# Ten of 32 destination blocks summed from gathered rows, 64-slot halves in pass 2, and one 384-wide product per source block

## The chip, the cores and the metric

The kernel runs on one core of a Trainium2 chip. The metric is device time in microseconds (us), smaller is better. Each kernel was timed in several rounds beside the kernel before on the same chip. A profiled execution has a span of its own, which is within about 1% of the median of the timed runs.

Names used below: PE multiplies matrices (PEld is its weight load), DVE does vector arithmetic, ACT does copies and activations, POOL issues the indirect DMAs, SP issues the other DMAs. PSUM is the memory into which PE writes its sums.

## The reference

```python
def reference(node_features, edge_index_src, edge_index_dst):     # 4096 nodes x 128, 65536 edges
    output = np.zeros((num_nodes, dim), dtype=np.float32)
    for i in range(len(edge_index_src)):
        output[edge_index_dst[i]] += node_features[edge_index_src[i]]
    return output
```

## The kernel before

The 4096 nodes are 32 blocks of 128. Two sorting passes, built from one-hot products, bring the edges into an order in which each pair of a destination block and a source block has its own columns. Then every destination block is *dense*: for each of 32 source blocks, PE makes the 128 x 128 count matrix of edges from two one-hots (`blocks`), and multiplies it with the features of the source block (`product`). Features are held as three bf16 parts whose sum is the float32 value, hence three products.

```python
    def blocks(k, oh, a):                       # PE -> psa, ACT copies it to a
        psa = ps.tile([P, 1024], F32, name="psa", tag="psA")
        for i in range(8):
            s = k * 8 + i
            PE.matmul(out=psa[:, i * P:(i + 1) * P], lhsT=oh[0][:, s, :], rhs=oh[1][:, s, :],
                      start=True, stop=True)
        S.copy(out=a[:, k * 8:k * 8 + 8, :], in_=psa[:].rearrange("p (s m) -> p s m", s=8))

    def product(k, a, pso):
        for s in range(k * 8, k * 8 + 8):
            for v in range(3):
                PE.matmul(out=pso[:, :P], lhsT=a[:, s, :], rhs=x3[:, s, v, :],
                          start=s == 0 and v == 0, stop=s == NB - 1 and v == 2)

    def finish(d, pso):
        res = sb2.tile([P, P], F32, name="res")
        S.copy(out=res[:], in_=pso[:, :P])      # ACT
        nc.sync.dma_start(out=out[d * P:(d + 1) * P, :], in_=res[:])
    # ... (cut) pass2(g), a generator, prepares the keys of the next 8 destination blocks
    for d in range(NB):
        # ... (cut) a new generator gen every 8 blocks
        oh = onehots(d)                         # two DVE instructions, 128 x 4096
        if gen is not None:
            next(gen, None)                     # one step of pass 2 for the next group
        a = sb2.tile([P, NB, P], BF16, name="a", tag="t1")
        pso = ps.tile([P, 512], F32, name="pso", tag="pso")
        for k in range(4):
            blocks(k, oh, a)
            if prev is not None:
                product(k, prev[1], prev[2])    # of the block before
        if prev is not None:
            finish(prev[0], prev[2])
        prev = (d, a, pso)
```

The instructions of each engine are issued in the order of this program. So what stands first on DVE is done first, even if a later instruction could already run.

## Time and profile before

| | before |
|---|---|
| median of timed runs | 508.5 us |
| span of the profile, mean granted PE clock | 507.9 us, 0.818 |
| first count-matrix product of the dense stage | at 180.4 us |
| from there to the end | 327.5 us |
| period of a settled dense block | 7.15 us |

From the page of the kernel before: the chain that ended last by engine, and its costliest groups. The columns of a group are line, engine, operation, output and inputs, shapes and count; then busy us and mean ns of one; then the idle us of the engine just before the group, and what ended most of it.

```profile
PE 59%; DVE 31%; issue 5%; ACT 3%; DMA 1%; DVEq 0%; ACTq 0%
...
L293 PE MATMUL pso<-x,a 128*128 128x128 bf16 x3072 | 200.2, 224 | 0.0
...
L176 DVE TENSOR_TENSOR p<-iota,rank 128x3072 bf16<-128x3072 uint16 (+1 forms) x38 | 90.8, 2426 | 24.3 <-PE ps L251 24.3
L276 DVE TENSOR_TENSOR oh<-iotas,slo 128x4096 bf16<-128x4096 uint16 x32 | 73.2, 2289 | 45.1 <-PE psa L286 45.1
L286 PE MATMUL psa<-oh 128*128 128x128 bf16 x1024 | 81.8, 226 | 1.3 <-ACT a L288 1.3
...
L232 PE MATMUL psr<-cum,identb 128*128 128x192 bf16 x128 | 20.2, 354 | 32.8 <-DVE cum L229 32.8
```

PE has 59% of the chain. Before the dense one-hots `oh`, DVE sits idle for 45.1 us in all *waiting for PE*, and PE hardly waits for anything before `psa` (1.3 us): DVE is ahead, PE sets the pace.

A settled block in the timeline of the kernel before (start us, length us, engine, line and operation; in brackets the idle time before it and its releaser):

```profile
461.68 2.29 DVE L276 TENSOR_TENSOR oh<-iotas,slo 128x4096 bf16<-128x4096 uint16 x1 [2.65 <-PE psa L286]
...
463.06 0.27 ACT L298 COPY res<-pso 128x128 f32<-128x128 f32 x1 [0.37 <-PE pso L293]
...
463.27 1.50 PE L293 MATMUL pso<-x,a 128*128 128x128 bf16 x24
...
463.89 2.28 DVE L276 TENSOR_TENSOR oh<-iota,dlo 128x4096 bf16<-128x4096 uint16 x1
...
464.61 0.61 PE L286 MATMUL psa<-oh 128*128 128x128 bf16 x8
...
470.21 0.27 ACT L298 COPY res<-pso 128x128 f32<-128x128 f32 x1 [0.37 <-PE pso L293]
```

The two results `res` leave 7.15 us apart. In between PE never stops, and the one-hots of the next block (461.68 to 466.17) are made while PE works on this one. The result is taken out of PSUM by ACT, so DVE does not wait for it.

### The profile page before, as it was taken

The numbers are of one execution on the slowest core, as the hardware profiler recorded it, in microseconds if no ns is written. First come the engines' busy times: TensorE is split into PE (matmuls) and PEld (weight loads), VectorE is DVE, ScalarE is ACT, GpSimd is POOL, SyncE is SP. The second block draws the span as 40 slices with busy tenths as digits, with TensorE's granted clock in tenths as the row PEclk, the third lists the DMA queues.
The fourth block names the chain that finished last, engine by engine and source line by source line (L and its number), as shares of the span: only waits on it lengthen the run. The fifth ranks groups of instructions, "written<-read, shape, count | busy, mean of one in ns | idle before, by whom it ended". The sixth has DMA issues, their size and how long they took to land.

```text
span 507.9 us, 12335 instructions
## 1 busy us (share of the span) xinstructions
PE 375.5 (74%) x5709; PEld 358.5 (71%) x5709; DVE 366.0 (72%) x429; ACT 163.1 (32%) x213; POOL 1.5 (0%) x10
## 2 busy tenths in 40 slices
PE   0607574610339283999999499999949999999997
PEld 0305574610238283999999499999949999999996
DVE  5697999735859899566789956678995666655630
ACT  1001000045000050332656133265613326665652
POOL 1000000000000000000000000000000000000000
PEclk9957766665665596987999798799979879999999
DMA  5000000011000000000000000000000000000000
GB/s 165 1 0 1 1 1 0 1 43 41 0 0 1 2 1 5 8 6 3 12 14 8 5 8 6 3 12 13 8 5 8 7 2 13 13 9 12 12 13 14
DMA packets 9109, 6.05 MB, mean 12 GB/s; under 512 B 608, under 2 KB 8800, under 8 KB 9056
## 3 DMA queue, kind: packets, MB, share of 16 engines
q1 hardware_dynamic: 8912, 4.72, 3.3%
q8 instruction: 45, 0.74, 0.6%
q10 hardware_dynamic: 144, 0.52, 0.3%
q14 instruction: 8, 0.07, 0.0%
HBM read 3.15 MB, written 2.10 MB: 10 GB/s over the span
## 4 chain that ended last, share of the span: by engine, by line
PE 59%; DVE 31%; issue 5%; ACT 3%; DMA 1%; DVEq 0%; ACTq 0%
PE pso L293 32%; PE psa L286 11%; DVE p L176 9%; DVE cum L228 5%; PE ps L251 5%; PE psr L232 4%; DVE oh L276 4%; PE psb L219 3%; DVE cum L229 3%; DVE v L141 2%; DVE cum L152 2%; ACT x L202 2%; DVE xf L204 2%; PE psr L160 2%; PE psb L131 2%
## 5 line engine op out<-in xcount | busy, mean ns | idle before, releaser
L293 PE MATMUL pso<-x,a 128*128 128x128 bf16 x3072 | 200.2, 224 | 0.0
L293 PEld LDWEIGHTS <-a 128*128 128x128 bf16 x3072 | 185.3, 100 | 0.0
L288 ACT CAST a<-psa 128x1024 bf16<-128x1024 f32 x128 | 129.2, 1013 | 87.3 <-PE psa L286 87.0
L176 DVE TENSOR_TENSOR p<-iota,rank 128x3072 bf16<-128x3072 uint16 (+1 forms) x38 | 90.8, 2426 | 24.3 <-PE ps L251 24.3
L276 DVE TENSOR_TENSOR oh<-iotas,slo 128x4096 bf16<-128x4096 uint16 x32 | 73.2, 2289 | 45.1 <-PE psa L286 45.1
L286 PE MATMUL psa<-oh 128*128 128x128 bf16 x1024 | 81.8, 226 | 1.3 <-ACT a L288 1.3
L276 DVE TENSOR_TENSOR oh<-iota,dlo 128x4096 bf16<-128x4096 uint16 x32 | 73.1, 2284 | 0.0
L286 PEld LDWEIGHTS <-oh 128*128 128x128 bf16 x1024 | 65.9, 101 | 1.7 <-issue 1.6
L251 PE MATMUL ps<-ov,p 128*128 128x32 bf16 x768 | 50.2, 238 | 6.7 <-DVE p L176 6.0
L251 PEld LDWEIGHTS <-p 128*128 128x128 bf16 x768 | 46.1, 120 | 10.2 <-DVE p L176 10.2
L190 PE MATMUL psm<-v,p 128*128 128x64 bf16 x512 | 31.7, 239 | 23.6 <-DVE p L176 23.1
L190 PEld LDWEIGHTS <-p 128*128 128x128 bf16 x512 | 30.6, 123 | 24.7 <-DVE p L176 24.7
L232 PE MATMUL psr<-cum,identb 128*128 128x192 bf16 x128 | 20.2, 354 | 32.8 <-DVE cum L229 32.8
L232 PEld LDWEIGHTS <-identb 128*128 128x128 bf16 x128 | 18.3, 144 | 34.7 <-issue 21.8
L219 PE MATMUL psb<-ov,before 128*128 128x256 bf16 x96 | 14.5, 322 | 35.2 <-DVE ov L215 35.2
L219 PEld LDWEIGHTS <-before 128*128 128x128 bf16 x96 | 10.9, 115 | 38.2 <-issue 26.0
L228 DVE TENSOR_TENSOR cum<-cum,ov 128x256 bf16<-128x256 bf16 x92 | 26.8, 291 | 4.4 <-ACT cum L222 1.4
L160 PE MATMUL psr<-cum,identb 128*128 128x264 bf16 x64 | 9.7, 323 | 17.5 <-DVE cum L157 17.5
L204 DVE TENSOR_TENSOR xf<-xf,x 128x1024 f32<-128x1024 f32 x8 | 9.8, 1226 | 17.3 <-ACT x L202 17.3
L160 PEld LDWEIGHTS <-identb 128*128 128x128 bf16 x64 | 7.1, 112 | 20.2 <-DVE cum L157 17.9
L254 ACT CAST pa<-ps 128x128 bf16<-128x128 f32 x8 | 2.1, 266 | 53.2 <-PE ps L251 53.2
L236 ACT CAST rank<-psr 128x192 bf16<-128x192 f32 x8 | 2.5, 377 | 51.7 <-PE psr L232 51.7
(47 smaller groups left out, 146.7 us busy)
## 6 DMA issues: line engine op xcount, KB each, us to landing
xf<-in_node_features_dram SPq DMA_DIRECT2D x4, 512.0 KB, 5.1
out_dram<-res SPq DMA_DIRECT2D x32, 64.0 KB, 1.5
raw<-in_edge_index_src_dram ACTq DMA_DIRECT2D x1, 512.0 KB, 5.1
raw<-in_edge_index_dst_dram SPq DMA_DIRECT2D x1, 512.0 KB, 4.9
```

The source lines that it names most:

```text
L160: PE.matmul(out=psr[:, :HJ * NCH], lhsT=identb[:], rhs=cum1[:, js, :, b, :].rearrange("p j q l -> p (j q) l"), start=b == 0, stop=b == NB - 1)
L176: V.tensor_tensor(out=dst.rearrange("p i (m k) -> p i m k", k=2), in0=iota[:, None, :].to_broadcast([P, n, P]).rearrange("p i (m k) -> p i ...
L190: PE.matmul(out=psm[:, l * 64:(l + 1) * 64], lhsT=p1[:, j * 4 + l, :], rhs=v1[q][:, j, :, :, l].rearrange("p k b -> p (k b)"), start=j == ...
L204: V.tensor_tensor(out=xf[:], in0=xf[:], in1=x3[:, i:i + 8, v, :], op=OP.subtract)
L219: PE.matmul(out=psb2[:, :NB * GD], lhsT=before[:], rhs=oh2[:, c], start=c == 0, stop=c == NCH - 1)
L228: V.tensor_tensor(out=cum2[:, c], in0=cum2[:, c - 1], in1=oh2[:, c - 1], op=OP.add)
L232: PE.matmul(out=psr[:, :NCH * GD], lhsT=identb[:], rhs=cum2[:, :, s, :], start=s == 0, stop=s == NB - 1)
L251: PE.matmul(out=ps2[:, (d % 4) * NB:(d % 4 + 1) * NB], lhsT=p2[:, c, :], rhs=v2[:, c, :, d], start=c == 0, stop=c == NCH - 1)
L276: V.tensor_tensor(out=dst.rearrange("p i (m k) -> p i m k", k=2), in0=io[:, None, :].to_broadcast([P, NB, P]).rearrange("p i (m k) -> p i ...
L286: PE.matmul(out=psa[:, i * P:(i + 1) * P], lhsT=oh[0][:, s, :], rhs=oh[1][:, s, :], start=True, stop=True)
L288: S.copy(out=a[:, k * 8:k * 8 + 8, :], in_=psa[:].rearrange("p (s m) -> p s m", s=8))
L293: PE.matmul(out=pso[:, :P], lhsT=a[:, s, :], rhs=x3[:, s, v, :], start=s == 0 and v == 0, stop=s == NB - 1 and v == 2)
```

## The change

Intent: fewer dense blocks. The source rows of ten destination blocks are fetched from memory by indirect DMA and added up with small one-hot products, on a queue and an engine (POOL) that did next to nothing before (1.5 us). The other 22 stay dense, with one product of 384 columns in place of three of 128. Pass 2 works with two halves of 64 slots, with half the cumulative adds and narrower one-hots, in eight smaller steps; the counts of pass 1 move from DVE to PE. The core of the diff (most of pass 1 is cut):

```diff
+    def gather(d, q):                                   # 60 tiles, 240 indirect DMAs
+        t = xg.tile([P, 4, 3 * P], BF16, name="rows", tag="xg")
+        for l in range(4):
+            G.indirect_dma_start(
+                out=t[:, l, :], out_offset=None, in_=x3d[:, :],
+                in_offset=bass.IndirectOffsetOnAxis(ap=gidx[:, place(q).start + l, d:d + 1], axis=0))
+        rows[d, q] = t
+    def gather_sum(d, q):
+        oh = sb2.tile([P, 4, P], BF16, name="ohg", bufs=6)
+        onehot(oh[:], gkey[:, place(q), d, :], 4)
         ...
+        for l in range(4):
+            PE.matmul(out=psg[d][:, :3 * P], lhsT=oh[:, l, :], rhs=t[:, l, :],
+                      start=q == 0 and l == 0, stop=q == NQ - 1 and l == 3)
+        if q == NQ - 1:
+            finish(d, psg.pop(d))
     def finish(d, pso):
-        S.copy(out=res[:], in_=pso[:, :P])
+        V.tensor_reduce(out=res[:], in_=pso[:, :3 * P].rearrange("p (v f) -> p f v", v=3),
+                        op=OP.add, axis=AX.X)
     ... pass 2, per destination block d of the group:
-                p2 = sb2.tile([P, NCH, P], BF16, name="p2")
-                onehot(p2[:], rank2[:, d], NCH)
+            p2 = p2b[d % 2]
+            for h in range(2):
+                cs = slice(h * NH, (h + 1) * NH)
+                onehot(p2[:, cs, h * 64:h * 64 + 64], rank2[:, d, cs], NH, 64)
     ... product:
-            for v in range(3):
-                PE.matmul(out=pso[:, :P], lhsT=a[:, s, :], rhs=x3[:, s, v, :], ...)
+            PE.matmul(out=pso[:, :3 * P], lhsT=a[:, s, :],
+                      rhs=x3[:, s, :, :].rearrange("p v f -> p (v f)"), ...)
     ... the dense loop:
+            oh = onehots(g, i)
+            while done < -(-STEPS * (i + 1) // gd):
+                next(gen, None)
+                done += 1
             for k in range(4):
                 blocks(k, oh, a)
                 if prev is not None:
                     product(k, prev[1], prev[2])
+                if prev is not None and k == 3:
+                    finish(prev[0], prev[2])
+            add_up(n0 + (len(order) - n0) * slot // slots)      # gather() and gather_sum()
```

`finish` is now a DVE instruction. In DVE's order it stands ahead of the one-hots of the next block.

## The prediction

> **What bounds the kernel now.** Span 507.9 us. By the chain of waits in time order and the timeline: 0-104 us first pass, DVE-bound (one-hot p 6.0 us plus two spreads of 1.62 us per quad, 9.0 us a quad); to 125 us the x split, ACT and DVE in turn; to 167 us the first second-pass group, exposed; then 340 us for 32 dense blocks, PE-bound. A settled dense block costs PE 7.15 us: four times eight block products (0.45 us) and 24 x 128-wide products (1.34 us, 55.8 ns each). Three groups also carry a second pass and take 89 us instead of 57. DVE makes the two one-hots (oh, 4.49 us) ahead and waits for PE (45.1 us).
>
> **What the change moves.**
> - Dense blocks: 32 to 22. Products 96 x 128 wide become 32 x 384 wide: the 128x384 matmuls here run at 160 ns warm, so PE per block is still about 7.0 us. It saves almost nothing by itself.
> - The result is now summed by a DVE reduce (0.55 us for 384 columns, as fmax) instead of an ACT copy. In DVE's order it stands BEFORE the next block's one-hots, and waits for the last product. DVE then does reduce 0.55, two gather one-hots (estimate 0.42 each from the 3072 and 4096 sizes), oh 4.49; PE can't start the next block until that ends. So PE and DVE alternate: 7.0 + 6.0 = 13.0 us a block, against 7.15.
> - The Trainium skill, "TensorE: Matmul & The Clock Gate", Part 1, says an idle window of about 3.4 us halves the PE clock. This trace agrees: after a gap of 6.86 us, 32 matmuls of 192 columns took 5.07 us, 158 ns each, then full speed. The new gap (6 us, 1.3 us of gather products inside) will cost an estimated 0.5 to 2 us per block.
> - Pass 2 halves: p2 3072 elements (1.72 us) to twice 768 (estimate 1.15 us); cum adds 23 to 11. But p2 and its products stand between oh and the block products: estimate 15 us exposed per later group.
> - Pass 1: cumulative counts go to PE (172 matmuls) and ACT copies. Each odd step waits for the previous step's copy, so a pair costs about 1.9 us warm: two halves of 21-30 us, the second ahead of the first move products. I estimate pass 1 ends at 148 us (before: 125 including the split), dense work starts near 178 (before 167).
> - 240 indirect DMAs on POOL. No trace here times one; "DMA: Bandwidth & Descriptors", latency table, gives about 1 us to first byte. From about 84 us they fit unless one costs over 1.8 us.
>
> **Sum.** 178 + 22 x 13.0-15 + 31 (p2) + 10 (eight gather reduces) + 13 (first and last) = 518-562. Since such a change was presumably tuned, I shade down: 527 us, 8 in 10 within 470-580. Faster 0.27, same 0.17, slower 0.56.
>
> **What would show it.** Per dense block a period of 13-15 us, PE idle some 5-6 us, released by DVE oh; DVE idle before the reduce res<-pso, released by PE; granted clock below the 0.9-1.0 of the old dense stage; PE busy down by about 80 us without span; count stage over 45 us.
>
> **What would make it wrong.** An indirect DMA above 1.8 us (POOL busy throughout, PE waiting for rows: slower still), or stalls of POOL under DVE; a shorter gap than computed, or pass 1 well under 140 us (faster); the clock staying full (518 or less).

## The result and the profile after

| | before | after |
|---|---|---|
| median of timed runs | 508.5 us | 608.0 us |
| span, mean granted PE clock | 507.9 us, 0.818 | 604.1 us, 0.793 |
| first count-matrix product | 180.4 us | 228.4 us |
| from there to the end | 327.5 us | 375.7 us |
| period of a late dense block | 7.15 us | 15.4 us |
| POOL busy | 1.5 us | 344.4 us |

The ratio is 1.196 (95% interval 1.189 to 1.202). A ratio here is the mean time of one kernel's fast runs over that of the other's fast runs of the same rounds, so it is not quite the ratio of the medians quoted. The prediction, 527 us within 470 to 580, was wrong in size: the loss was foreseen as the likelier side, but 608 us lies outside the range. So 100 us are to be explained, 81 more than predicted.

From the page of the kernel after, the chain by engine and the groups that answer to those above (line numbers are those of the new file; 239 is the line of a helper that makes all one-hots):

```profile
PE 43%; DVE 25%; another core or an unknown queue 13%; issue 9%; ACT 5%; POOL 2%; DMA 1%; DVEq 0%; ACTq 0%
...
L286 POOL DMA_INDIRECT rows<-x3d,gidx x240 | 310.9, 1295 | 212.8 <-PE psg L300 99.0
L434 PE MATMUL pso<-x,a 128*128 128x384 bf16 x704 | 152.1, 368 | 0.0
...
L307 DVE TENSOR_REDUCE res<-pso 128x128 f32<-128x384 f32 x22 | 12.3, 557 | 191.0 <-PE pso L434 173.7
L428 PE MATMUL psa<-oh 128*128 128x128 bf16 x704 | 64.8, 244 | 50.9 <-DVE oh L239 45.3
...
L239 DVE TENSOR_TENSOR oh<-iotas,slo 128x4096 bf16<-128x4096 uint16 x22 | 50.2, 2283 | 0.0
```

The direction of the waiting has turned. DVE sits idle for 191.0 us before its reduces, nearly all until PE ends a product, and PE waits 45.3 us for DVE's one-hots. Each waits for the other in turn. PE's products fell from 200.2 us for 32 blocks to 152.1 us for 22, but nothing of that shows in the span.

One late block in the timeline of the kernel after:

```profile
494.25 0.56 DVE L307 TENSOR_REDUCE res<-pso 128x128 f32<-128x384 f32 x1 [9.76 <-PE pso L434]
494.72 0.75 DVE L239 TENSOR_TENSOR ohg<-iota,gkey 128x512 bf16<-128x512 uint16 x2
...
495.19 1.47 PE L300 MATMUL psg<-rows,ohg 128*128 128x384 bf16 x8 [2.03 <-DVE ohg L239]
495.39 2.28 DVE L239 TENSOR_TENSOR oh<-iotas,slo 128x4096 bf16<-128x4096 uint16 x1
...
497.59 2.28 DVE L239 TENSOR_TENSOR oh<-iota,dlo 128x4096 bf16<-128x4096 uint16 x1
...
499.93 0.62 PE L428 MATMUL psa<-oh 128*128 128x128 bf16 x8 [3.27 <-DVE oh L239]
...
500.39 1.95 PE L434 MATMUL pso<-x,a 128*128 128x384 bf16 x8
...
507.30 1.46 PE L434 MATMUL pso<-x,a 128*128 128x384 bf16 x8
...
509.68 0.56 DVE L307 TENSOR_REDUCE res<-pso 128x128 f32<-128x384 f32 x1 [9.81 <-PE pso L434]
```

The reduce at 494.25 had waited 9.76 us for PE. Only then come the gather one-hots and the one-hots of the next block, and PE's next `psa` starts at 499.93, after 3.27 us idle. PE is done at 508.8 us by its record, yet the reduce that waits for it starts at 509.68. From reduce to reduce it is 15.4 us (14.5 to 16.9 in the last full blocks). This is the alternation the prediction describes.

There is a second thing that it does not describe. Here is PE before the dense stage, with POOL beside it, in the timeline of the kernel after:

```profile
192.12 0.95 POOL L286 DMA_INDIRECT rows<-x3d,gidx  x1 [0.30 <-issue]
193.00 0.30 PE L397 MATMUL ps<-v,p2b 128*128 128x32 bf16 x3 [1.08 <-issue]
...
193.37 0.95 POOL L286 DMA_INDIRECT rows<-x3d,gidx  x1 [0.30 <-issue]
193.75 0.20 PE L397 MATMUL ps<-v,p2b 128*128 128x32 bf16 x1 [0.46 <-issue]
...
194.47 0.29 PE L397 MATMUL ps<-v,p2b 128*128 128x32 bf16 x3 [0.51 <-issue]
194.62 0.94 POOL L286 DMA_INDIRECT rows<-x3d,gidx  x1 [0.30 <-issue]
195.18 0.20 PE L397 MATMUL ps<-v,p2b 128*128 128x32 bf16 x1 [0.42 <-issue]
195.87 0.95 POOL L286 DMA_INDIRECT rows<-x3d,gidx  x1 [0.30 <-issue]
...
196.59 0.30 PE L397 MATMUL ps<-v,p2b 128*128 128x32 bf16 x3 [1.20 <-issue]
```

PE issues matmuls by ones to threes (the count at the end of the line) with gaps of 0.4 to 1.2 us. The releaser is "issue": the profile shows no semaphore that PE waits for, and its operands are ready. Meanwhile POOL issues one indirect DMA every 1.25 us. In all, PE idles 22.0 us in this way in the kernel after, and never in the kernel before.

The trace has another sign of it. Of the PE instructions of the kernel after that signal another engine, 63 of 425 have their next signal on record over 0.3 us later than the end that the trace models for them; in the kernel before 0 of 207 do. I call these *late completions*. Overlapping ones merged, they last 89.8 us in all in this trace. (An end is modelled and the time includes stalls off the critical path, so this is a detector and not a cost. It also counts too much: where there are many indirect DMAs, some signals have no record. The trace of the kernel after holds 405, that of x6, with the same 425 instructions, 428. A missing one is read as late until the next.) A check that needs no such record is the ACT copy of `psa`: in 17 of 88 cases in the kernel after it starts over 0.5 us later than both PE's modelled end and ACT's own last work, 34.5 us in all, and in none of 128 in the kernel before.

### The profile page after: what moved, and what is told of

It reads as the page before. It is cut to its first block, busy times and chain, and to the rows that moved or that the text cites. A ratio compares the mean times of both kernels' runs of the same rounds, so it can differ in the third digit from the quotient of the medians.

```text
span 604.1 us, 7564 instructions
## 1 busy us (share of the span) xinstructions
PE 379.6 (63%) x3151; PEld 251.2 (42%) x3151; DVE 294.9 (49%) x491; ACT 131.2 (22%) x182; POOL 344.4 (57%) x263
## 3 DMA queue, kind: packets, MB, share of 16 engines
q0 software_dynamic: 11520, 23.61, 15.5%
## 4 chain that ended last, share of the span: by engine, by line
PE 43%; DVE 25%; another core or an unknown queue 13%; issue 9%; ACT 5%; POOL 2%; DMA 1%; DVEq 0%; ACTq 0%
PE pso L434 21%; DVE oh L239 13%; PE psa L428 8%; PE psc L191 4%; PE ps L397 3%; PE psg L300 2%; DVE ohg L239 2%; ACT cum L192 2%; PE psm L252 2%; POOL rows L286 2%; PE psr L384 2%; DVE oh L143 1%; DVE cum L377 1%; ACT x L163 1%
## 5 line engine op out<-in xcount | busy, mean ns | idle before, releaser
L286 POOL DMA_INDIRECT rows<-x3d,gidx x240 | 310.9, 1295 | 212.8 <-PE psg L300 99.0
L434 PE MATMUL pso<-x,a 128*128 128x384 bf16 x704 | 152.1, 368 | 0.0
L430 ACT CAST a<-psa 128x1024 bf16<-128x1024 f32 x88 | 88.3, 1015 | 249.9 <-PE psa L428 193.8
L300 PE MATMUL psg<-rows,ohg 128*128 128x384 bf16 x240 | 60.8, 394 | 86.9 <-DVE ohg L239 59.8
L307 DVE TENSOR_REDUCE res<-pso 128x128 f32<-128x384 f32 x22 | 12.3, 557 | 191.0 <-PE pso L434 173.7
L428 PE MATMUL psa<-oh 128*128 128x128 bf16 x704 | 64.8, 244 | 50.9 <-DVE oh L239 45.3
L434 PEld LDWEIGHTS <-a 128*128 128x128 bf16 x704 | 73.7, 110 | 47.3 <-issue 20.1
L397 PE MATMUL ps<-v,p2b 128*128 128x32 bf16 x528 | 34.2, 233 | 26.9 <-DVE p2b L239 14.3
L239 DVE TENSOR_TENSOR oh<-iotas,slo 128x4096 bf16<-128x4096 uint16 x22 | 50.2, 2283 | 0.0
L239 DVE TENSOR_TENSOR oh<-iota,dlo 128x4096 bf16<-128x4096 uint16 x22 | 50.2, 2283 | 0.0
L397 PEld LDWEIGHTS <-p2b 128*128 128x128 bf16 x528 | 30.4, 122 | 32.0 <-DVE p2b L239 16.1
L239 DVE TENSOR_TENSOR p<-iota,rank 128x2816 bf16<-128x2816 uint16 x24 | 37.4, 1618 | 5.7 <-issue 3.0
L252 PEld LDWEIGHTS <-p 128*128 128x128 bf16 x512 | 31.1, 121 | 10.1 <-DVE p L239 7.5
L165 POOL TENSOR_TENSOR xf<-xf,x 128x1024 f32<-128x1024 f32 x8 | 29.0, 3646 | 8.4 <-ACT x L163 8.4
```

What stands on the lines that cost most here:

```text
L165: G.tensor_tensor(out=xf[i][:], in0=xf[i][:], in1=x3[:, i * BX:(i + 1) * BX, v, :], op=OP.subtract)
L239: V.tensor_tensor(out=dst.rearrange("p i (m k) -> p i m k", k=2), in0=io.rearrange("p i (m k) -> p i m k", k=2), in1=keys2[:, :, None, :]. ...
L252: PE.matmul(out=psm[:, l * 64:(l + 1) * 64], lhsT=p1[:, l % 2, j, :], rhs=v1[q][:, j, :, :, l].rearrange("p k b -> p (k b)"), start=j == j ...
L286: G.indirect_dma_start(out=t[:, l, :], out_offset=None, in_=x3d[:, :], in_offset=bass.IndirectOffsetOnAxis(ap=gidx[:, place(q).start + l, ...
L300: PE.matmul(out=psg[d][:, :3 * P], lhsT=oh[:, l, :], rhs=t[:, l, :], start=q == 0 and l == 0, stop=q == NQ - 1 and l == 3)
L307: V.tensor_reduce(out=res[:], in_=pso[:, :3 * P].rearrange("p (v f) -> p f v", v=3), op=OP.add, axis=AX.X)
```

## The experiments

Two theories were open from the start. *Order*: the reduce on DVE stands ahead of the next one-hots and makes PE and DVE alternate. *Gathers*: the indirect DMAs hold up PE, POOL or the rows. Seventeen kernels were run. Kernels marked "wrong" give a wrong result but do the same kinds of work. The kernel before took 508.7 to 509.6 us beside them. The table gives medians; "late" is the merged time of late completions in the profiled run, too large where records are missing, and "issue" is the time that PE idles there with no releaser known.

| run | base | edit | us | ratio | late, us | issue, us |
|---|---|---|---|---|---|---|
| x1_reduce_later | after | reduce behind next one-hots | 577.7 | 1.127 | 115.1 | 51.0 |
| x2_no_gather | after | 24 of 240 gathers | 555.8 | 1.089 | 6.1 | 0 |
| x3_before_wide | before | 384-wide, DVE reduce first | 723.5 | 1.419 | 0 | 0 |
| x4_before_wide_late | before | 384-wide, reduce later | 543.4 | 1.066 | 0 | 0 |
| x5_both | after | x1 and x2 | 478.5 | 0.939 | 4.8 | 0 |
| x6_sp_rows | after | plain DMAs, SP queue | 548.9 | 1.078 | 0 | 0 |
| x7_pool_rows | after | plain DMAs, POOL queue | 551.4 | 1.081 | 0 | 0 |
| x8_rows256 | after | a third of the bytes | 611.7 | 1.199 | 88.5 | 23.2 |
| x9_consecutive | after | consecutive rows | 605.7 | 1.190 | 73.3 | 26.2 |
| x10_wide_after_gen | before | x4, reduce later still | 514.1 | 1.007 | 0 | 0 |
| x11_halves_wide | before | x10 and halves | 6625 | 13.0 | | |
| x12_half | x1 | 132 gathers | 499.4 | 0.977 | 29.3 | 10.6 |
| x13_halves_mended | before | x11 mended | 469.3 | 0.921 | 0 | 0 |
| x14_halves_alone | before | halves only | 469.6 | 0.926 | 0 | 0 |
| x15_one_in_four | x1 | 60 indirect, 180 plain | 478.4 | 0.939 | 0 | 0 |
| x16_memset_between | x1 | memset between gathers | 575.3 | 1.131 | 102.4 | 45.0 |
| x17_plain_between | x12 | plain DMA between gathers | 494.9 | 0.971 | 36.2 | 0 |

### Order and gathers, one at a time and both

x1 undoes only the order: `finish` of a dense block is emitted after the next block's one-hots. Correct.

```diff
+    pend = []
+    def flush():
+        for p in pend:
+            finish(*p)
+        pend.clear()
 ...
             oh = onehots(g, i)
+            flush()
 ...
-                    finish(prev[0], prev[2])
+                    pend.append((prev[0], prev[2]))
```

> The kernel after, with only the order changed on DVE: the reduce of a dense block (and of a gathered block where it can wait) is given to DVE after the next block's one-hots instead of before them. Theory A (PE and DVE alternate because of that order): the settled dense slot falls from 15.4 us to 9 to 11 us, PE no longer waits for oh, the time falls by 70 to 110 us to 500-540 us. Rival B (the excess is stalls that come with the gathers, whatever the order): under 25 us gained, 580 us or more.

Measured 577.7 us: 30 us better, short of what order alone foretold. Late completions grew to 115.1 us, and the late copies of `psa` from 34.5 to 70.2 us. With the alternation gone, the fastest blocks take 8.3 to 9.6 us. Six take 24 to 43 us; the same six take 14 to 23 us in x5 below, so not all of that is the gathers. The timeline of x1 shows one such stall:

```profile
442.97 0.61 PE L428 MATMUL psa<-oh 128*128 128x128 bf16 x8 [1.27 <-ACT a L430]
...
445.89 0.95 POOL L286 DMA_INDIRECT rows<-x3d,gidx  x1 [0.30 <-issue]
...
446.81 0.48 PE L434 MATMUL pso<-x,a 128*128 128x384 bf16 x1 [0.82 <-issue]
447.14 0.94 POOL L286 DMA_INDIRECT rows<-x3d,gidx  x1 [0.30 <-issue]
...
447.52 0.49 PE L434 MATMUL pso<-x,a 128*128 128x384 bf16 x1 [0.23 <-issue]
...
448.39 0.95 POOL L286 DMA_INDIRECT rows<-x3d,gidx  x1 [0.30 <-issue]
451.80 1.93 ACT L430 CAST a<-psa 128x1024 bf16<-128x1024 f32 x2 [8.88 <-remote]
```

PE's product `psa` at 442.97 lasts 0.61 us; the ACT copy of it starts at 451.80 (listed as "remote": the profile knows no releaser), after the stretch of indirect DMAs has ended at 449.34. So order was hiding some of the gathers' cost, and the two do not add.

x2 undoes only the gathers: after the first six tiles, the tiles already there are used again, so 24 indirect DMAs are left of 240. Its output is wrong, which doesn't matter for the time.

```diff
     def gather(d, q):
+        if len(made) >= 6:
+            rows[d, q] = made[len(rows_seen) % 6]
+            rows_seen.append(1)
+            return
         t = xg.tile([P, 4, 3 * P], BF16, name="rows", tag="xg")
+        made.append(t)
```

> The kernel after with 24 of its 240 indirect DMAs; the other 54 groups read the first six row tiles again (wrong result on purpose), every other instruction kept. If the gathers add stalls (rows that come late in pass 1, PE whose completions are signalled late), the time falls by 50 to 80 us to 525-555 us, which was the upper half of the predicted sum without such stalls, dense slots go from 15.4 to about 14 us, and the waits on an unknown releaser vanish. If those waits have nothing to do with the gathers, it stays within 10 us of 608.

Measured 555.8 us, just outside the band. The gathers cost 52 us in after's order. The last full blocks still take 14.2 to 17.1 us. So the alternation is there without the gathers.

x5 takes both away (the two diffs above together; wrong).

> Reduce after the next one-hots (as the first experiment) and 24 of 240 indirect DMAs (as the second; wrong result on purpose). The two singly gave 578 and 556 us against 608. If they add, 525 us. If the gathers hide what the order costs (the stalls with gathers fill the gaps that the order would free), more than the sum is gained: 460 to 495 us, settled dense slots of 9 to 10 us, PE completions within 0.3 us of the modelled end.

Measured 478.5 us, a hit. From x2 to x5 order is worth 77 us. From x1 to x5 the gathers are worth 99 us. In x5 the waits have turned back:

```profile
L434 PE MATMUL psa<-oh 128*128 128x128 bf16 x704 | 60.5, 236 | 22.4 <-DVE oh L239 21.5 <-ACT a L436 1.0
...
L313 DVE TENSOR_REDUCE res<-pso 128x128 f32<-128x384 f32 x22 | 12.2, 556 | 41.6 <-PE pso L440 41.5
```

DVE's wait before the reduces of dense blocks fell from 191.0 to 41.6 us, PE's wait for `oh` from 45.3 to 21.5.

### The order by itself, on the kernel before

x3 gives the kernel before the 384-wide product and the reduce in the place where the change has it, no gathers. Correct.

```diff
-            for v in range(3):
-                PE.matmul(out=pso[:, :P], lhsT=a[:, s, :], rhs=x3[:, s, v, :],
-                          start=s == 0 and v == 0, stop=s == NB - 1 and v == 2)
+            PE.matmul(out=pso[:, :3 * P], lhsT=a[:, s, :],
+                      rhs=x3[:, s, :, :].rearrange("p v f -> p (v f)"),
+                      start=s == 0, stop=s == NB - 1)
-        S.copy(out=res[:], in_=pso[:, :P])
+        V.tensor_reduce(out=res[:], in_=pso[:, :3 * P].rearrange("p (v f) -> p f v", v=3),
+                        op=OP.add, axis=AX.X)
```

> The kernel before with only the 384-wide product and the DVE reduce of the result, in the order that the change has (reduce before the next one-hots); no gathers, no halves. Theory A: the last group's blocks go from 7.15 us to about 12 us each and PE waits for oh in each; 590 to 640 us in all. Rival B: within 15 us of before.

Measured 723.5 us, more than expected: a miss in size. Settled blocks take 13.7 us, which is the alternation, but those that carry a step of pass 2 take 20 to 27 us, since the pass-2 one-hots, too, now stand behind the reduce. The group of the reduces in x3:

```profile
L298 DVE TENSOR_REDUCE res<-pso 128x128 f32<-128x384 f32 x32 | 17.8, 558 | 287.1 <-PE pso L292 287.1
```

DVE stands still for 287.1 us before 32 reduces of 0.56 us. Besides the wide product nothing else was changed, and x10 below has that product without the loss.

x4 emits the reduce after the next block's one-hots. Correct.

```diff
         oh = onehots(d)
+        if late is not None:
+            finish(*late)
+            late = None
         if gen is not None:
             next(gen, None)
 ...
-            finish(prev[0], prev[2])
+            late = (prev[0], prev[2])
```

> As x3, with the reduce given to DVE after the next one-hots. Theory A: the settled block is back at 7.0 to 7.3 us and the time at 498 to 515 us. If the wide product or the reduce itself is what costs, it stays near x3.

Measured 543.4 us, not 498 to 515. Two settled reduces of x4 in its timeline:

```profile
484.13 0.56 DVE L298 TENSOR_REDUCE res<-pso 128x128 f32<-128x384 f32 x1 [2.03 <-PE pso L292]
...
491.12 0.56 DVE L298 TENSOR_REDUCE res<-pso 128x128 f32<-128x384 f32 x1 [2.03 <-PE pso L292]
```

A settled block takes 6.99 us, as expected. The miss is in blocks with pass 2: there the reduce now stands ahead of the pass-2 step's one-hots. x10 moves it behind that step too (the three added lines after `next(gen, None)`). Correct.

> The kernel before with the 384-wide product and the DVE reduce emitted after the next block's one-hots and after that slot's pass-2 step. Order theory: then nothing PE needs stands behind the reduce, all slots are as before, settled slot 7.0 us: 497-507 us. Rival, the DVE reduce of PSUM costs the pass-2 slots by itself: 520 us or more.

Measured 514.1 us, ratio 1.007: outside the band, by 7 us, but not the rival's 520. With the reduce where it holds up nothing needed at once, the 384-wide product neither gains nor loses by 2%. In this sequence only the place of one 0.56 us instruction changes: 723.5, 543.4, 514.1 us.

### What it is about the gathers

x6 and x7 fetch the same bytes in the same places of the program by plain DMAs, from SP's queue and from POOL's. Their outputs are wrong, which doesn't matter for the times. The line in its place is, for x7 (x6 has `nc.sync` for `G`):

```diff
-            G.indirect_dma_start(
-                out=t[:, l, :], out_offset=None, in_=x3d[:, :],
-                in_offset=bass.IndirectOffsetOnAxis(ap=gidx[:, place(q).start + l, d:d + 1], axis=0))
+            G.dma_start(out=t[:, l, :], in_=x3d[(4 * d + l) % 32 * P:((4 * d + l) % 32 + 1) * P, :])
```

> The kernel after with each indirect DMA replaced by a plain DMA of the same 128 rows of 768 bytes on SP's queue (neighbouring rows, wrong result on purpose). If the bytes moved into SBUF delay PE, the long lags of PE's completions stay and the time is 595 to 610 us. If it is POOL's issue of indirect DMAs[...], the lags vanish and the time is 545 to 565 us, near the run without gathers.

> As x6, with the plain DMAs on POOL's queue. If any DMA that POOL issues does it, as slow as the change (595 to 620 us); if only data-dependent row addresses do, as x6.

Measured 548.9 and 551.4 us, no late completion in either. x7 moved as many packets (11520) and bytes (23.61 MB) on POOL's queue as the kernel after did. So it is not the traffic, and not that POOL issues a DMA at all. The group in x7, to be set against the 1295 ns of an indirect DMA:

```profile
L286 POOL DMA_DIRECT2D rows<-x3d x240 | 129.2, 546 | 335.7 <-PE psg L298 320.9 <-DMA x3d<-x 8.3 <-issue 4.2
```

x7 also says where the 52 us go. Its first `psa` is at 194.0 us and the rest of its span takes 357.7 us; the kernel after has 228.4 and 375.7. So 34 us are lost before the dense stage and 18 in it. Of the 34, 28 are in the first group of pass 2, where PE was seen to issue by ones to threes: from its first one-hot to the first dense one-hot it is 34.0 us in x7 (147.3 to 181.3) and 62.0 us in the kernel after (153.1 to 215.1).

x8 fetches 256 bytes a row in place of 768; x9 fetches 128 consecutive rows by the same instruction. Their outputs are wrong, which doesn't matter for the times.

```diff
 x8:
-                out=t[:, l, :], out_offset=None, in_=x3d[:, :],
+                out=t[:, l, :P], out_offset=None,
+                in_=x3d[:, :].rearrange("n (v f) -> (n v) f", v=3),
 x9:
-        V.tensor_scalar(out=gidx[:, cs, :], in0=gt3[:], scalar1=-float(P + (CODE0 >> 7)),
-                        scalar2=0.0, op0=OP.add, op1=OP.max)
+        V.scalar_tensor_tensor(out=gidx[:, cs, :], in0=gt3[:], scalar=0.0,
+                               in1=rowf[:, cs, None].to_broadcast([P, 4, KG]),   # row 128c + p
+                               op0=OP.mult, op1=OP.add)
```

> Indirect DMAs of 256-byte rows in place of 768 (same count of DMAs and rows; the product reads the 128 columns three times, wrong result on purpose). If POOL's issue or the count of rows is what costs, within 10 us of 608. If the bytes are, 30 us or more faster.

> The kernel after with all 240 indirect DMAs kept, but each now fetches 128 consecutive rows (row number 128c + p) instead of scattered ones; results wrong on purpose. If it is the scattered rows in HBM that hold PE up: 545-560 us as with plain DMAs, almost no late PE completions. If it is the kind of instruction, an indirect DMA whatever it fetches: 600-615 us, 50-70 late PE completions, POOL still near 1.3 us a DMA.

Measured 611.7 and 605.7 us, both as expected of the kind of instruction, with 88.5 and 73.3 us of late completions and 23.2 and 26.2 us of issue gaps. Neither the bytes nor the scatter of the rows matters. It is the indirect DMA itself.

x12 drops every other gather tile of x1 and reads the tile before it again: 132 indirect DMAs. Its output is wrong, which doesn't matter for the time.

```diff
+        calls.append(1)
+        if len(made) >= 6 and len(calls) % 2:
+            rows[d, q] = made[-1]
+            return
```

> As x1 (reduce after the next one-hots) with every other gather replaced by reading the tile gathered before, so about half of the indirect DMAs (132 of 240); wrong on purpose. If each indirect DMA costs PE about the same (578 against 478 us for 240 against 24: 0.46 us each): 522-535 us, late PE completions about half of 77. If only a crowded POOL queue does it (back-to-back DMAs): under 500 us.

Measured 499.4 us: below the proportional band, and by a hair within the rival's. 24, 132 and 240 indirect DMAs give 478.5, 499.4 and 577.7 us: the first 108 more cost 21 us, the next 108 cost 78. The 21 us are all lost before the dense stage: the first `psa` is at 216.6 us (x5: 195.7), and from there to the end it takes 283.0 us (x5: 281.0). All 21 merged late completions of x12 (missing records included) lie within or at most 3 us after a stretch of indirect DMAs issued one behind the other. Such windows cover 286 of its 500 us.

x15 keeps one indirect DMA in each tile of x1 and makes the other three plain, on the same queue. Its output is wrong, which doesn't matter for the time.

```diff
+            if l > 0:
+                G.dma_start(out=t[:, l, :], in_=x3d[(4 * d + l) % 32 * P:((4 * d + l) % 32 + 1) * P, :])
+                continue
             G.indirect_dma_start(
```

> As x1 (reduce after the next one-hots), but of each tile's four row fetches only the first is an indirect DMA, the other three are plain DMAs of the same bytes on the same queue; wrong on purpose. 60 indirect DMAs, never two in a row. If each indirect DMA costs PE about the 0.2 us that it did in x12: 488-500 us, late PE completions adding up to 10-20 us. If only stretches of several in a row do it: 476-487 us, under 5 us of late completions.

Measured 478.4 us, no late completion and no issue gap: 60 indirect DMAs cost no more than x5's 24. Two starts of indirect DMAs are at least 2.92 us apart there. The timeline of POOL in x15:

```profile
155.49 1.01 POOL L289 DMA_INDIRECT rows<-x3d,gidx  x1 [0.30 <-issue]
156.49 1.63 POOL L287 DMA_DIRECT2D rows<-x3d  x3
158.42 3.26 POOL L289 DMA_INDIRECT rows<-x3d,gidx  x1 [0.30 <-DMA rows<-x3d,gidx]
```

That left two readings: the direct succession of two indirect DMAs, or how many are under way in a given time. x16 puts a POOL memset of one element per partition behind each of the 240 (correct); x17 splits each of x12's into an indirect DMA of 96 rows and a plain one of 32 behind it (wrong).

```diff
 x16:
             G.indirect_dma_start(...)
+            G.memset(pause[:], 0.0)
 x17:
-                out=t[:, l, :], ...  ap=gidx[:, ...
+                out=t[:96, l, :], ... ap=gidx[:96, ...
+            G.dma_start(out=t[96:, l, :], in_=x3d[l * P:l * P + 32, :])
```

> As x1 (reduce after the next one-hots, all 240 indirect DMAs, correct), with a POOL memset of one element per partition (about 0.1 us) after every indirect DMA. If the direct succession of two of them holds PE up: late PE completions nearly gone, 480-510 us. If it is how many are under way, or the memset does not part them: 570-590 us, late completions as in x1 (115 us merged).

> As x12 (132 indirect DMAs, wrong on purpose), each indirect DMA fetching 96 rows and followed by a plain DMA on the same queue for the other 32. If the direct succession holds PE up: late completions under 5 us against 29 us in x12, about 480-490 us. If it is how many are under way: late completions 15 us or more, 495-510 us.

Measured 575.3 and 494.9 us; the second lies between the two bands. In x16 the hold-up stays as in x1: issue gaps of 45.0 us (51.0), late copies of `psa` of 60.5 us (70.2). But the memset fits into the 0.30 us between two indirect DMAs. They still start 1.25 us apart at the closest, so x16 leaves their rate as it was. The timeline of POOL in x17:

```profile
166.39 0.95 POOL L293 DMA_INDIRECT rows<-x3d,gidx  x1 [0.30 <-issue]
167.34 0.56 POOL L296 DMA_DIRECT2D rows<-x3d  x1
168.20 0.95 POOL L293 DMA_INDIRECT rows<-x3d,gidx  x1 [0.30 <-issue]
```

Here the detector misleads. x17 shows 36.2 us of late completions, but its trace holds 251 of some 279 signals, and the engine that waits mostly starts at once. The late completion of x17 that looks longest, 4.81 us, is that of this `psa`, which ends at 258.14; the copy of it starts at 258.18:

```profile
257.53 0.61 PE L436 MATMUL psa<-oh 128*128 128x128 bf16 x8
...
258.18 1.01 ACT L438 CAST a<-psa 128x1024 bf16<-128x1024 f32 x1 [1.45 <-issue]
```

No copy of `psa` is over 0.5 us late in x17, and PE has no issue gap. So, by these signs, PE is not held up in it. What it loses against x5 comes before the dense stage (first `psa` at 213.0 us against 195.7; from there to the end 283.0 against 281.0), where PE waits 16.7 us for the plain rows of its tiles (x5: no such wait).

One indirect DMA every 1.25 us at the closest holds PE up; one every 1.80 us (x17) or 2.92 us (x15) at the closest does not, in these kernels. Their rate fits all runs. So does another reading: a plain DMA in between parts them (x15, x17) and a memset does not (x16). x17's also fetch 96 rows and not 128. No run separates these, and what PE and the indirect DMAs share was not found.

### The third part: the 64-slot halves

x11 adds to x10 the pass 2 of the change (its generator, word for word but for names), with all 32 blocks dense and no gathers.

> As x10, and the pass 2 of the kernel after (64-slot halves: 11 instead of 23 cumulative adds, p2 one-hots of 64 columns), no gathers, all 32 blocks dense, correct. The halves take some 18 us of p2 one-hots and 12 adds off DVE in each of four groups; only the first group is exposed in full (42 us before): 478-497 us. If pass 2's DVE work was hidden anyway and its eight-step spread costs PE waits: 500 us or more.

Measured 6625 us, correct. This is the kernel's fallback: a flag is raised if a half holds over 64 entries, and then everything is done again by a slow general path. By my count of the input, which no trace shows, I had kept the old order of the 24 chunks, and with it the fullest half has 65 entries. The change deals the chunks to the halves in turn by quads, which are four chunks, and its fullest has 56. That x13 below needs no fallback agrees with it. In the trace of x11 the fast path ends at 462.6 us. x13 is x11 with the chunks dealt out as in the change; x14 has only the halves, with 128-wide products and the ACT copy. Both correct.

```diff
 x13, against x11:
-        S.copy(out=sa[:, q * 4:q * 4 + 4, :], in_=pv[:, :, 0, :])
-        S.copy(out=sbk[:, q * 4:q * 4 + 4, :], in_=pv[:, :, 1, :])
+        at = (q % 2 * (NQ // 2) + q // 2) * 4
+        S.copy(out=sa[:, at:at + 4, :], in_=pv[:, :, 0, :])
+        S.copy(out=sbk[:, at:at + 4, :], in_=pv[:, :, 1, :])
 x14, against x13: product() and finish() as in the kernel before
```

> As x11, with the chunks dealt to the halves in turn by quads, as the kernel after does, so that no half holds over 64 (56 by a count of the input); correct. The fast path of x11's trace ended at 462.6 us before its fallback began. If the halves gain and the order is mended: 458-472 us. If the fallback's trace misleads and the halves do not pay: 495 us or more.

> The kernel before with only the 64-slot halves of pass 2 (128-wide products, result copied by ACT); correct. If the gain is the halves' alone: within 8 us of x13, 458-480 us. If the wide product and the moved reduce are needed for it: 485 us or more.

Measured 469.3 and 469.6 us, ratios 0.921 and 0.926: hits, and both beat the kernel before and the kernel after. The groups of x14 that answer to L176 and L232 of the kernel before:

```profile
L181 DVE TENSOR_TENSOR p2b<-iota,rank 128x768 bf16<-128x768 uint16 x64 | 32.3, 555 | 33.1 <-PE ps L260 19.0 <-ACT rank L251 14.1
...
L247 PE MATMUL psr<-cum,identb 128*128 128x192 bf16 x128 | 12.6, 263 | 9.3 <-DVE cum L243 9.3
```

The 32 pass-2 one-hots of 3072 elements took 1754 ns each in the kernel before. Now two of 555 ns take 1.11 us a block. PE's wait before `psr` fell from 32.8 to 9.3 us. A group of eight blocks with pass 2 takes 77.9 us (from result 215.5 to 293.4), before 88.8 us (211.3 to 300.1), and there are three such groups. The first result comes 10.3 us earlier (181.0 against 191.3). Three times 10.9 and 10.3 are 43 us; the two spans, 507.9 and 466.6, are 41.3 us apart. The halves and the finer steps (eight in place of five) came together; they were not run apart.

## Why the prediction was wrong

- **What bounds the kernel before: right.** DVE waits for PE, 7.15 us a block.
- **PE and DVE alternate, 13.0 to 15 us a block: right in mechanism, and nearly in size.** After has 15.4 us; x3, which has nothing but this order, 13.7 us; x2, nearly without gathers, 14.2 to 17.1 us. Moving the reduce takes it away (x4, x5). The clock part rests on the Trainium skill, "TensorE: Matmul & The Clock Gate", Part 1, on an idle window of about 3.4 us halving the clock. This trace agrees in kind: PE idles some 2.9 to 3.6 us before most dense blocks until `oh` is made, and the granted clock falls to 0.5 for stretches of 3 to 14 us. In x3 the gap is 5.05 us, the clock is 0.5 for 3.4 us of every settled block, and the block takes 13.7 us where 13.0 were computed without it. So an estimate of 0.5 to 2 us per block was fair.
- **The wide product saves almost nothing: right.** 6.99 against 7.15 us a block (x4), 514.1 us in all (x10).
- **Pass 1 later by 11 us: right without the gathers, wrong with them.** x7's first `psa` is 13.6 us later than before. The kernel after's is 48 us later. Pass 1 itself ends where it was predicted to (148 us): pass 2 starts at 147.3 us in x7 and at 125.3 in the kernel before.
- **"240 indirect DMAs on POOL ... they fit unless one costs over 1.8 us": this is the step that failed.** One costs 1.295 us and 0.30 us to the next, under that limit. So by that criterion they fit, and still they cost 52 us (608.0 against 555.8 in x2 and 551.4 in x7), and 99 us once the order is mended. The step counted POOL's time and nothing for PE. What the runs showed in its place: indirect DMAs that follow each other every 1.25 us hold up PE's issue (22.0 us of gaps, none in x7) and its completions (`psa` copied 34.5 us late in all, never in x7), whatever they fetch (x8, x9). PE's waits for rows are the smaller part: 8.4 us in the kernel after, none in x7. The prediction named "stalls of POOL under DVE" as a danger; POOL's are there too, but PE's were not thought of.
- **The sum, 518 to 562, was right for a kernel without that term.** x2, x6 and x7 are it: 548.9 to 555.8 us.
- **"Since such a change was presumably tuned, I shade down": wrong.** It moved the value 13 us or more away from a sum that the trace supported. Adding the unseen 52 us to the sum gives 570 to 614, which holds 608.
- **PE busy down by about 80 us: wrong.** The page has 379.6 us after and 375.5 before. Products, count matrices and pass-2 products did fall by 81 us together (200.2, 81.8 and 50.2 to 152.1, 64.8 and 34.2). But the gather products (60.8 us) and the counts moved to PE (33.3 us; its four kinds of product overlap, and add up to 56.8) were not set against that. It costs no time here, as PE is not what binds, but it shows what ten gathered blocks save on PE: little.
- **The halves: not named as a gain.** The sum carried 31 us for pass 2 in the later new groups, where three old ones take 89 us in place of 57, but what the halves gain by themselves was not worked out. They are worth 39 us alone.

Whether gathers could pay with the order mended: x5 and x15, whose gathers hold PE up little or not at all, take 478 us; x14, with no gather at all, 469.6 us. A version with nearly free gathers has not beaten the dense one here. But that is not the gathers' doing alone. From the first `psa` to the end x5 takes 281.0 us and x14 301.1, so fewer dense blocks save 20 us there. x5 loses 30 us earlier (first `psa` at 195.7 us against 165.4), most of it in pass 1: pass 2 starts at 148.8 us against 125.1. The counts of pass 1 on PE, a fourth part of the change, were never run alone, nor apart from the gather products that PE does in that time.

Left open: what indirect DMAs and PE share, whether it is their rate or what stands between them that counts, and what the new pass 1 costs by itself. The losses of 52 and 99 us are those of the timed medians; the late completions and the slow issue are read from the traces alone. Every timed run lists a granted clock too, so none is known to have been taken without the profiler, and that its recording has a part in the hold-up is not ruled out.

## What to carry to other kernels

When the instruction that empties an accumulator is moved to another engine, look at what that engine has to do next in program order: one 0.56 us reduce ahead of the next block's one-hots cost 209 us in x3 against x10, which has it later. Cost a new kind of instruction for every engine around it, not only for the one that issues it, and test it with a twin that does the same work by known means (here plain DMAs of the same bytes). When a change bundles several parts, run each alone: here the 64-slot halves carried a gain of 7%, and the rest hid it.

## What the Trainium skill lacked or had wrong

- "SBUF — State Buffer", Who interferes with whom, says that DMA never contends with a compute engine, and that PE and ACT never wait on anyone. That section has nothing on PE being held up beside indirect DMAs: 22.0 us of PE's issue gaps in the kernel after, 51.0 in x1, none with plain DMAs of the same bytes (x6, x7). The runs do not show that it is SBUF that they share.
- The same section says that a DVE instruction with two SBUF inputs contends with a GpSimd instruction that reads SBUF. The kernel after agrees in kind: 109 indirect DMAs with no DVE instruction beside them took 0.95 us each at the most, 131 with one (of over 0.15 us) took 1.59 us in the mean and up to 5.0. Plain DMAs do not show it: in x7 they took 0.55 us in the mean with a DVE tensor_tensor beside them and without. The page gives no size for indirect ones.
- "DMA: Bandwidth & Descriptors", Latency and other measured facts, gives about 1 us to the first byte for a DMA from GpSimd, and no figure for what an indirect one costs POOL: 1295 ns in the mean and 0.30 us to the next, against 546 ns for a plain one (x7).
- No page has a limit to the rate of indirect DMAs: stretches with one every 1.25 us held PE up, none did where they started 1.80 us (x17) or 2.92 us (x15) or more apart. That the rate alone decides is not shown.
- "GPSIMD Engine Reference", Performance versus the Vector engine, gives 1.96 for the time of a float32 add of two tensors on GpSimd over that on DVE. Here the subtract of 128 x 1024 bf16 values from float32 ones took POOL 3646 ns in the mean in the kernel after and DVE 1226 ns in the kernel before, 3.0 times as long. But DVE was at work beside six of the eight; the two without took 2.12 us, 1.7 times as long. The page's ratio has no word for a busy DVE.
